# One shared set of 13 weight buffers with deeper splitting at the joints, and an in-place residual, in a two-block transformer kernel

## The chip, the cores and the metric

The kernel runs on one core of a Trainium2 chip. The metric is the device time of one execution in microseconds (us); the number given for a kernel is the median of several executions. The engines are named as in the profile: PE is TensorE (matrix multiplication), DVE is VectorE, ACT is ScalarE, POOL is GpSimd and SP is SyncE, whose queue issues the loads of the weights.

## The reference

256 tokens of width 1024 in float32 pass through two blocks. The joins between the stages are of two kinds: block 1 normalises after the sum (deep-norm, LayerNorm), block 2 normalises a branch with RMS, adds it, and normalises again ahead of the next branch.

```
block 1:  x = LN(alpha*x + retention(x));        x = LN(alpha*x + swiglu(x))
          x = LN(alpha*x + stick_breaking(x));   x = LN(alpha*x + moe_swiglu(x))   # 8 experts, top 2
block 2:  for l in 0, 1:
            x = x + RMS(hybrid_mixer_l(RMS(x)*mix_pre_g))*mix_post_g
            x = x + RMS(conv_ffn_l(RMS(x)*ffn_pre_g))*ffn_post_g
```

The time goes into the products with the weights: 519 MB of them, each used once.

## The kernel before

**Units.** Every weight matrix is cut into units of 1 MB (128 partitions x 2048 float32), numbered here U0 to U518 in the order of use: retention 0 to 31 (the last 8 are its output projection), ffn 32 to 64 (output projection from 54), stick-breaking attention 65 to 80, MoE 81 to 416, and then in block 2 hybrid mixer 0 (417 to 434), conv-ffn 0 (435 to 467, output projection from 457), hybrid mixer 1 (468 to 485) and conv-ffn 1 (486 to 518). To reach float32 accuracy a unit is used as two parts: SP loads the raw unit (`raw`, line 64), ACT copies it with rounding into `wh` (line 74), DVE subtracts to get the rest, `wl` (line 85), and PE forms three products, wh with xh, wl with xh, wh with xl, where xh and xl are the activation split in the same way (lines 191 and 192).

**The stream.** The class `Stream` keeps this going. Python code written in order decides which engine gets which instruction next; nothing is reordered later, and each engine, SP's queue among them, takes its instructions in that order. `get` hands PE the next split unit, `done` marks it as used, `advance` emits as many splits as allowed (at most `pairs` units split and not yet done) and as many loads as there are buffers. Raw units have 4 buffers of their own, split parts 8 (4 pairs; 3 pairs in the MoE, where further buffers are lent for raws).

**The joints.** `proj_out` (line 236) runs a stage's output projection, one unit after the other, with `advance` after each. Its last four units are the `tail` (line 248): all four for token half 0, then `joint.stats(0)`, then all four for token half 1, with `joint.trans(0)` ahead of the end, then `joint.stats(1)`. `stats(t)` adds and normalises the residual of a token half on DVE and ACT; `trans(t)` lets PE transpose it (line 1294), and ACT and DVE split it into xh and xl. `head` (line 269) then starts the next stage: four units for token half 0, with `trans(1)` ahead of the fourth, then the four for token half 1. So PE meets two places where it may have to wait: the head's first unit, which needs xh and xl of half 0, and `trans(1)`, which needs stats(1). In `tail` `advance` stands ahead of stats(0), after the units named in `joint.early`, and, where `joint.after` is set, behind stats(1).

The joint between retention and ffn is called ret to ffn, and so on: ffn to stick, stick to MoE, MoE to hyb0, hyb0 to conv-ffn0, conv-ffn0 to hyb1, hyb1 to conv-ffn1. The joints ret to ffn, ffn to stick, conv-ffn0 to hyb1 and the end come behind `proj_out`; the other stages call `tail` by themselves.

**The normalisations.** `LayerNorm.stats` (line 1317): z = alpha*x + acc and its statistics (lines 1326 and 1327), then per half of the columns z = (z - mean)*g and x = z*rs + b (1314, 1315), with rs from ACT's square root and DVE's reciprocal (317). `RmsNorm.stats` (line 1377): ACT squares acc (1384), then per column half z = acc*rs*g (1388) and x = z + x (1389); `pre` (1345) forms the next stage's input z. The residual x has two buffers that take turns.

Of the kernel before, what the change touches and what calls it, by code (L numbers as in the profile page):

```python
# [16 lines left out]
OP = mybir.AluOpType  # L17
# [15 lines left out]
class Stream:  # L33


    def __init__(self, nc, pool, pairs, raws, units):
        self.nc, self.pool, self.units = nc, pool, units
        self.pairs = self.room = pairs
        self.free = [(pool, "raw%d" % i, len(units)) for i in range(raws)]
        self.n_load = self.n_h = self.n_l = self.n_get = self.n_done = 0  # L40
        self.rt, self.ht = {}, {}

    def widen(self, slots):

        self.free = slots + self.free

    def slot(self):
        return next((s for s in self.free if self.n_load < s[2]), None)

    def raw(self, s):  # L50
        self.free.remove(s)
        if s[1] == "part":
            return s[0].tile([128, UNIT], F32, tag="part", name="raw", bufs=2 * self.room)
        return s[0].tile([128, UNIT], F32, tag=s[1], name="raw")

    def part(self, name):
        return self.pool.tile([128, UNIT], F32R, tag="part", name=name, bufs=2 * self.room)

    def load(self):
        s = self.slot()  # L60
        if s is None or self.n_load >= len(self.units):
            return False
        t = self.raw(s)
        self.nc.sync.dma_start(t, self.units[self.n_load])
        self.rt[self.n_load] = (t, s)
        self.n_load += 1
        return True

    def split_h(self):
# [3 lines left out]
        h = self.part("wh")  # L73
        self.nc.scalar.activation(h, self.rt[i][0], AF.Copy)  # L74
        self.ht[i] = h
        self.n_h += 1
        return True

    def split_l(self):
        i = self.n_l  # L80
        if i >= self.n_h:
            return False
        (r, s), h = self.rt.pop(i), self.ht[i]
        l = self.part("wl")
        self.nc.vector.tensor_tensor(l, r, h.bitcast(F32), op=OP.subtract)  # L85
        self.ht[i] = (h, l)
        self.free.append(s)
        self.n_l += 1
        self.load()
        return True  # L90

    def advance(self):
        while self.split_h():
            self.split_l()
        while self.split_l():
            pass
        while self.load():
            pass

    def get(self):  # L100
        i = self.n_get
# [5 lines left out]
        return self.ht.pop(i)  # L107

    def done(self):
        self.n_done += 1  # L110


# [10 lines left out]


class Net:
    PAIRS, RAWS = 4, 4

    def __init__(self, ctx, tc, a):
        self.ctx, self.tc, self.nc, self.a = ctx, tc, tc.nc, a

        def pool(name, bufs, **k):
            return ctx.enter_context(tc.tile_pool(name=name, bufs=bufs, **k))

        self.ring = pool("ring", 1)
        self.gl, self.xt, self.xT = pool("gl", 1), pool("xt", 1), pool("xT", 1)
        self.x_tag = 0
        self.sm = pool("sm", 2)
        self.ps = pool("ps", 1, space=PSUM)
        ctx.enter_context(tc.manual_schedule())

    def prepare(self, units):
        self.W = Stream(self.nc, self.ring, self.PAIRS, self.RAWS, units)

    def psA(self):
        return self.ps.tile([128, 2, 512], F32, tag="A", name="pa", bufs=2)
# [12 lines left out]
    def consts(self):  # L158
# [21 lines left out]
    def new_x(self):  # L180
        self.x_tag ^= 1
        self.x = self.xt.tile([128, 2, D], F32, tag="x%d" % self.x_tag, name="x")
        return self.x

    def new_xT(self):
        xh = self.xT.tile([128, KC, S], F32R, tag="xh", name="xh")
# [49 lines left out]
    def proj_out(self, yh, yl, n, joint):  # L236

        accs = [self.psA(), self.psA()]
        m = 4
        for u in range(n - m):  # L240
            w = self.W.get()
            for t in range(2):
                self.out_unit(accs[t], w, yh, yl, u, t, u == 0, False)
            self.W.done()
            self.W.advance()
        self.tail(accs, [(yh, yl, u) for u in range(n - m, n)], n == m, joint)

    def tail(self, accs, items, first, joint, hooks=()):
        m = len(items)
        ws = [self.W.get() for _ in range(m)]  # L250
        for i, (yh, yl, u) in enumerate(items):
            if i < len(hooks):
                hooks[i]()
            self.out_unit(accs[0], ws[i], yh, yl, u, 0, first and i == 0, i == m - 1)
        self.W.advance()
        joint.stats(0, accs[0])
        accs[1] = accs[1] or self.psA()
        for i, (yh, yl, u) in enumerate(items):
            self.out_unit(accs[1], ws[i], yh, yl, u, 1, first and i == 0, i == m - 1)
            self.W.done()  # L260
            if i == m - 2:
                joint.trans(0)
            if i in joint.early:
                self.W.advance()
        joint.stats(1, accs[1])
        if joint.after:
            self.W.advance()

    def head(self, joint, table, n=4):

        ws, ps = [], []
        for i in range(n):
            if i == n - 1:
                joint.trans(1)
                self.nc.scalar.preload_act_table_set(table + "_and_others")
            ws.append(self.get8())
            ps.append(self.psP([128, 2, 256]))
            self.tokB(ps[i], ws[i], 0)
        for i in range(n):
            self.tokB(ps[i], ws[i], 1)  # L280
            self.W.done()
            yield ps[i]
# [37 lines left out]
    def start(self):  # L320
        nc, a = self.nc, self.a
        self.xh, self.xl = self.new_xT()
        W = self.W
        sx, sw = W.free[:2]
        xr, t, h, l = W.raw(sx), W.raw(sw), W.part("wh"), W.part("wl")
# [9 lines left out]
        W.ht[0] = (h, l)  # L335
        W.free += [sx, sw]
        W.n_load = W.n_h = W.n_l = 1
        W.advance()
        nc.sync.dma_start(self.new_x(), a["x"])

    def rotary(self, ps, out, cos, sin, scale, pool):
        nc = self.nc
# [114 lines left out]
    def stick(self, joint0):  # L457
# [106 lines left out]
        between(6)  # L564
        parts(7)
        joint = LayerNorm(self, o, w, 2, "kT")
        joint.early = (0, 1, 2)
        joint.after = False

        def last():  # L570
            pv(6)
# [8 lines left out]
    def open_moe(self):  # L580

        W = self.W
        self.mp = p = self.span.enter_context(self.tc.tile_pool(name="m1", bufs=1))
        self.moe_i = i = W.n_get
        end = i + 6 * E * SL
        W.widen([(p, "yy", i + 44)] + [(p, "more%d" % j, end) for j in range(2)])
        while W.load():
            pass

    def moe(self, joint0):  # L590
        nc, tc, a, W = self.nc, self.tc, self.a, self.W
        with self.span:
            p, o = self.mp, self.shared
            end = self.moe_i + 6 * E * SL
            W.widen([(self.xt, "x%d" % (self.x_tag ^ 1), self.moe_i + 46)])
            W.load()
# [51 lines left out]
            W.widen([(self.ring, "part", end - 8)] * 2)  # L648
            while W.load():
                pass  # L650
            route(0)
            low_part(1, nc.vector)
            route(1)
# [193 lines left out]
            for st in [(e, s) for e in range(E) for s in range(SL)] + [None]:  # L847
# [19 lines left out]
                if prev is not None:  # L867
                    hh, hl = parts()
                    turn(prev[2], hh, hl)
                    if st is None:  # L870
                        joint = MoeNorm(self, o, p, 3, 0)
                        W.pairs = 4
                        W.advance()
                if st is not None and e in (1, 3, 5) and s > 4:
                    gather_step(e // 2 + 1, 2 * s - 10, True)
                if part is not None and s == 1:
                    if acc is None:
                        acc = self.new_x()
# [423 lines left out]
class LayerNorm(Joint):  # L1302
# [66 lines left out]
class RmsNorm(Joint, PreNorm):  # L1369
# [7 lines left out]
    def stats(self, t, acc):  # L1377
# [171 lines left out]
```

## Time and profile before

| what | value |
|---|---|
| median of 3 executions | 2299.37 us (2298.87 to 2300.28) |
| the profiled execution: time | 2301.24 us |
| its span in the profile | 2299.5 us |
| mean granted clock of TensorE | 0.986 of full speed |
| DMA: packets, bytes, mean rate | 80074, 562.07 MB, 244 GB/s |
| wl subtractions (DVE, line 85) | 518 |
| matrix instructions on PE | 13077 |

The span is the time from the first to the last instruction in the trace; the profiled execution's own time is 1.74 us longer and 1.87 us above the median. Rows of the trace give an instruction's start and its duration in us; in square brackets stands how long the engine was idle just before, and which instruction ended that. A mean granted clock of 1 would be 2.4 GHz all the time; where it falls, it falls to 1.2 GHz.

### The profile page before, as it was taken

The numbers are of one execution on the slowest core, as the hardware profiler recorded it, in microseconds if no ns is written. First come the engines' busy times: TensorE is split into PE (matmuls) and PEld (weight loads), VectorE is DVE, ScalarE is ACT, GpSimd is POOL, SyncE is SP. The second block draws the span as 40 slices with busy tenths as digits, with TensorE's granted clock in tenths as the row PEclk, the third lists the DMA queues.
The fourth block names the chain that finished last, engine by engine and source line by source line (L and its number), as shares of the span: only waits on it lengthen the run. The fifth ranks groups of instructions, "written<-read, shape, count | busy, mean of one in ns | idle before, by whom it ended". The sixth has DMA issues, their size and how long they took to land. (4 is left out here: it accounts for less than half of the span.)

```text
span 2299.5 us, 31879 instructions
## 1 busy us (share of the span) xinstructions
PE 2220.5 (97%) x13077; PEld 1929.2 (84%) x13077; DVE 1711.3 (74%) x1670; ACT 1373.2 (60%) x1376; POOL 88.1 (4%) x87
## 2 busy tenths in 40 slices
PE   8999999997999999999999999997999999999998
PEld 8998998886888888888887888886888998888996
DVE  6565554656889888888888888997876975776973
ACT  4343443474777777777776777774555654555652
POOL 4000000010000000000000000300000000000000
PEclk9999999998999999999999999998999999999999
DMA  8444555436989799989997999985334554433551
GB/s 317 147 165 165 184 195 189 151 115 256 366 333 340 284 388 352 357 312 383 351 361 284 354 370 363 356 328 179 129 125 151 203 185 163 149 129 129 212 193 65
DMA packets 80074, 562.07 MB, mean 244 GB/s; under 512 B 9072, under 2 KB 9136, under 8 KB 13488
## 3 DMA queue, kind: packets, MB, share of 16 engines
q1 hardware_dynamic: 76464, 547.39, 64.3%
q0 software_dynamic: 3456, 12.55, 1.6%
q8 instruction: 105, 1.72, 0.3%
q14 instruction: 49, 0.40, 0.1%
HBM read 558.86 MB, written 1.05 MB: 243 GB/s over the span
## 5 line engine op out<-in xcount | busy, mean ns | idle before, releaser
L85 DVE TENSOR_TENSOR wl<-raw,wh 128x2048 fp32r<-128x2048 f32 x518 | 1187.8, 2300 | 312.7 <-ACT wh L74 295.1
L74 ACT ACTIVATE wh<-raw 128x2048 fp32r<-128x2048 f32 x518 | 990.9, 1916 | 397.3 <-PE pp L744 198.5
L197 PE MATMUL pp<-xh,wh 128*128 128x256 f32 x1360 | 387.3, 285 | 7.8 <-ACT wh L191 7.8
L197 PE MATMUL pp<-xh,wl 128*128 128x256 f32 x1360 | 386.9, 285 | 1.2 <-DVE wl L85 1.1
L197 PE MATMUL pp<-xl,wh 128*128 128x256 f32 x1360 | 384.1, 282 | 0.0
L197 PEld LDWEIGHTS pp<-xh,wh 128*128 128x128 f32 x1360 | 257.8, 190 | 9.1 <-ACT wh L191 8.1
L197 PEld LDWEIGHTS pp<-xl,wh 128*128 128x128 f32 x1360 | 258.6, 190 | 0.2 <-issue 0.2
L197 PEld LDWEIGHTS pp<-xh,wl 128*128 128x128 f32 x1360 | 255.9, 188 | 2.4 <-DVE wl L85 1.4
L197 PE MATMUL pp<-wl,xh 128*128 128x256 f32 x720 | 207.0, 288 | 7.8 <-DVE wl L85 7.8
L197 PE MATMUL pp<-wh,xh 128*128 128x256 f32 x720 | 210.6, 292 | 3.4 <-DVE mix L1132 3.2
L197 PE MATMUL pp<-wh,xl 128*128 128x256 f32 x720 | 206.0, 286 | 0.0
L744 PE MATMUL pp<-wh,xgh 128*128 128x512 f32 x448 | 179.4, 400 | 3.7 <-DVEq L821 3.7
L744 PE MATMUL pp<-wh,xh 128*128 128x512 f32 x448 | 179.5, 401 | 0.0
L744 PE MATMUL pp<-wl,xh 128*128 128x512 f32 x448 | 178.0, 397 | 0.5 <-DVE wl L85 0.5
L744 PE MATMUL pp<-wl,xgh 128*128 128x512 f32 x448 | 176.6, 394 | 1.5 <-DVE wl L85 1.5
L744 PE MATMUL pp<-wh,xl 128*128 128x512 f32 x448 | 177.7, 397 | 0.0
L744 PE MATMUL pp<-wh,xgl 128*128 128x512 f32 x448 | 176.8, 395 | 0.0
L197 PEld LDWEIGHTS pp<-wl,xh 128*128 128x128 f32 x720 | 140.4, 195 | 9.8 <-DVE wl L85 8.8
L197 PEld LDWEIGHTS pp<-wh,xh 128*128 128x128 f32 x720 | 140.1, 195 | 5.8 <-issue 4.2
L754 PE MATMUL pa<-wh,hh 128*128 128x512 f32 x448 | 142.2, 399 | 0.7 <-ACT hh L191 0.7
L754 PE MATMUL pa<-wl,hh 128*128 128x512 f32 x448 | 141.4, 397 | 0.0
L754 PE MATMUL pa<-wh,hl 128*128 128x512 f32 x448 | 141.4, 397 | 0.0
(337 smaller groups left out, 3089.2 us busy)
## 6 DMA issues: line engine op xcount, KB each, us to landing
raw<-in_moe_w_in SPq DMA_DIRECT2D x224, 1024.0 KB, 6.8
raw<-in_moe_w_out SPq DMA_DIRECT2D x112, 1024.0 KB, 6.6
raw<-in_w_up SPq DMA_DIRECT2D x44, 1024.0 KB, 4.8
raw<-in_w_in SPq DMA_DIRECT2D x28, 1024.0 KB, 4.9
raw<-in_ret_w_in SPq DMA_DIRECT2D x23, 1024.0 KB, 5.2
raw<-in_ffn_w_in SPq DMA_DIRECT2D x22, 1024.0 KB, 4.9
raw<-in_w_down SPq DMA_DIRECT2D x22, 1024.0 KB, 4.8
raw<-in_ffn_w_out SPq DMA_DIRECT2D x11, 1024.0 KB, 4.8
```

What stands on the lines that cost most here:

```text
L74: self.nc.scalar.activation(h, self.rt[i][0], AF.Copy)
L85: self.nc.vector.tensor_tensor(l, r, h.bitcast(F32), op=OP.subtract)
L197: self.nc.tensor.matmul(out, lhsT=w, rhs=x, start=(i == 0), stop=(i == n - 1))
L744: nc.tensor.matmul(q, lhsT=x[:, k, :], rhs=ww[:, kk, :], start=(k == 0 and i == 0), stop=(k == KC - 1 and i == 2))
L754: nc.tensor.matmul(A[0][f], lhsT=x[:, k, :], rhs=ww[:, kk, half(f)], start=(s == 0 and k == 0 and i == 0), stop=(s == SL - 1 and k == 3 an ...
```

## The change

- The raws and the split parts take their buffers from one list of 13 equal ones; before there were 4 for raws and 8 for parts. A load is issued only if the buffers that are then left are enough for the splits that are still to come before it.
- In the plain stages up to 5 units may be split ahead (`PAIRS`), from the start of `proj_out` up to 6 (`JOINT_PAIRS`), and from the head's end of its first pass on 5 again; in the MoE 3 as before.
- `advance` stands after the tail's units 0, 1 and 2 at every joint; behind stats(1) only loads are issued.
- The residual is updated in its place. One buffer of x is given up; the MoE's sum has a buffer of its own instead.
- `LayerNorm.norm`: the reciprocal comes behind the first z. `RmsNorm.stats`: DVE multiplies acc by the weight g while ACT forms the squares, and one instruction per column half then does x = z*rs + x.

PE's instructions, their order, and the order of the loads stay as they are.

```diff
-        self.free = [(pool, "raw%d" % i, len(units)) for i in range(raws)]
+        self.free = [(pool, "b%d" % i, len(units)) for i in range(count)]
...
+    def take(self, i, name, dt=F32R):
+        s = next((s for s in self.free if i < s[2]), None)
+        assert s is not None
         self.free.remove(s)
+        return s[0].tile([128, UNIT], dt, tag=s[1], name=name), s
+
+    def spare(self, i):
+        return sum(i < s[2] for s in self.free)

     def load(self):
+        i = self.n_load
+        if i >= len(self.units):
             return False
+        parts = max(0, min(i - self.n_h + 1, self.pairs - (self.n_h - self.n_done)))
+        if self.spare(i) <= parts + (parts > 0):
+            return False
+        t = self.rt[i] = self.take(i, "raw", F32)
+        self.nc.sync.dma_start(t[0], self.units[i])
         self.n_load += 1
         return True
...
 class Net:
-    PAIRS, RAWS = 4, 4
+    PAIRS, JOINT_PAIRS, BUFS = 5, 6, 13
...
     def proj_out(self, yh, yl, n, joint):
         accs = [self.psA(), self.psA()]
+        self.W.pairs = self.JOINT_PAIRS
...
         joint.stats(1, accs[1])
-        if joint.after:
-            self.W.advance()
+        self.W.fill()
...
             self.tokB(ps[i], ws[i], 0)
+        self.W.pairs = self.PAIRS
...
 class Joint:
-    early = (0, 2)
-    after = True
+    early = (0, 1, 2)
...
-        self.xo = n.x
-        self.xn = n.new_x()
+        self.xo = self.xn = n.x
...
-        r = n.rstd(mv[:, 1:2], n.eps_ln, 1.0)
+        sd = n.small(1, "rs_sd")
+        nc.scalar.activation(sd, mv[:, 1:2], AF.Sqrt, bias=n.eps_ln)
+        r = n.small(1, "rs")
         for f in range(2):
             s = half(f)
             nc.vector.scalar_tensor_tensor(z[:, s], z[:, s], mv[:, 0:1], self.g[:, s], op0=OP.subtract, op1=OP.mult)
+            if f == 0:
+                nc.vector.reciprocal(r, sd)
             nc.vector.scalar_tensor_tensor(dst[:, s], z[:, s], r, self.b[:, s], op0=OP.mult, op1=OP.add)
...
-        nc.scalar.activation(z, acc, AF.Square, accum_out=ss)
+        nc.scalar.activation(junk, acc, AF.Square, accum_out=ss)
+        for f in range(2):
+            nc.vector.tensor_tensor(z[:, half(f)], acc[:, half(f)], self.g[:, half(f)], op=OP.mult)
         r = n.rstd(ss, n.eps_rms, 1.0 / D)
         for f in range(2):
             s = half(f)
-            nc.vector.scalar_tensor_tensor(z[:, s], acc[:, s], r, self.g[:, s], op0=OP.mult, op1=OP.mult)
-            nc.vector.tensor_tensor(self.xn[:, t, s], z[:, s], self.xo[:, t, s], op=OP.add)
+            nc.vector.scalar_tensor_tensor(self.xn[:, t, s], z[:, s], r, self.xo[:, t, s], op0=OP.mult, op1=OP.add)
```

**How the order of instructions moves.** Three places, all on DVE; a row is a line of the kernel, the operation, what it writes and reads, and how often it comes in succession. The lines of the change are some 3 to 8 higher (wl is line 85 before and 93 after, xl 192 and 196). First the joint ffn to stick on DVE, from the run of subtractions of the output projection to those behind stats(0); before:

```order
L85 TENSOR_TENSOR wl<-raw,wh 128x2048 x8
L1326 SCALAR_TENSOR_TENSOR z<-x,pa 128x512
L1327 BN_STATS st<-z 128x6
L1326 SCALAR_TENSOR_TENSOR z<-x,pa 128x512
L1327 BN_STATS st<-z 128x6
L1310 BN_AGGR mv<-st 128x2
L317 RECIPROCAL rs<-rs_sd 128x1
L1314 SCALAR_TENSOR_TENSOR z<-z,mv,gains 128x512
L1315 SCALAR_TENSOR_TENSOR x<-z,rs,gains 128x512
L1314 SCALAR_TENSOR_TENSOR z<-z,mv,gains 128x512
L1315 SCALAR_TENSOR_TENSOR x<-z,rs,gains 128x512
L85 TENSOR_TENSOR wl<-raw,wh 128x2048
```

The same place on DVE with the change:

```order
L93 TENSOR_TENSOR wl<-raw,wh 128x2048 x9
L1329 SCALAR_TENSOR_TENSOR z<-x,pa 128x512
L1330 BN_STATS st<-z 128x6
L1329 SCALAR_TENSOR_TENSOR z<-x,pa 128x512
L1330 BN_STATS st<-z 128x6
L1309 BN_AGGR mv<-st 128x2
L1315 SCALAR_TENSOR_TENSOR z<-z,mv,gains 128x512
L1317 RECIPROCAL rs<-rs_sd 128x1
L1318 SCALAR_TENSOR_TENSOR x<-z,rs,gains 128x512
L1315 SCALAR_TENSOR_TENSOR z<-z,mv,gains 128x512
L1318 SCALAR_TENSOR_TENSOR x<-z,rs,gains 128x512
L93 TENSOR_TENSOR wl<-raw,wh 128x2048 x2
```

The run ahead of stats(0) goes from U57 to U64 before and from U58 to U66 now, and two subtractions, U67 and U68, follow it where one stood; the reciprocal has moved behind the first z.

Second the head's side of the joint ret to ffn on DVE, from the end of stats(0) to the start of stats(1); before:

```order
L1315 SCALAR_TENSOR_TENSOR x<-z,rs,gains 128x512
L85 TENSOR_TENSOR wl<-raw,wh 128x2048
L192 TENSOR_TENSOR xl<-pp,xh 128x4x128 x2
L85 TENSOR_TENSOR wl<-raw,wh 128x2048 x2
L1326 SCALAR_TENSOR_TENSOR z<-x,pa 128x512
```

The same place on DVE with the change:

```order
L1318 SCALAR_TENSOR_TENSOR x<-z,rs,gains 128x512
L93 TENSOR_TENSOR wl<-raw,wh 128x2048 x2
L196 TENSOR_TENSOR xl<-pp,xh 128x4x128 x2
L93 TENSOR_TENSOR wl<-raw,wh 128x2048
L1329 SCALAR_TENSOR_TENSOR z<-x,pa 128x512
```

Ahead of xl, which the head's first unit needs, stand two subtractions (U34 and U35) where one stood (U32), and one (U36) stands ahead of stats(1) where U33 and U34 stood. Behind stats(1), where U35's subtraction stood ahead of the next xl, none is left. ACT's copies wh have moved in the same way.

Third the joint MoE to hyb0 on DVE, from the first subtraction behind stats(0) to the additions for token half 1 (x, or acc with the change, gathers the experts' sum); before:

```order
L85 TENSOR_TENSOR wl<-raw,wh 128x2048
L192 TENSOR_TENSOR xl<-pp,xh 128x4x128 x2
L85 TENSOR_TENSOR wl<-raw,wh 128x2048
L796 TENSOR_TENSOR x<-pp,x 128x512 x2
L1364 BN_STATS st<-x 128x6 x2
```

The same place on DVE with the change:

```order
L93 TENSOR_TENSOR wl<-raw,wh 128x2048
L196 TENSOR_TENSOR xl<-pp,xh 128x4x128 x2
L93 TENSOR_TENSOR wl<-raw,wh 128x2048 x3
L797 TENSOR_TENSOR acc<-pp,acc 128x512 x2
L1367 BN_STATS st<-acc 128x6 x2
```

Three subtractions stand ahead of the additions where one stood; the other two (the first splits of hyb0) have come from ahead of stats(0).

## Rows read from the trace of the kernel before

**Rows 1.** The page, part 1: busy time (us), share of the span, instructions.

```profile
PE 2220.5 (97%) x13077; PEld 1929.2 (84%) x13077; DVE 1711.3 (74%) x1670; ACT 1373.2 (60%) x1376; POOL 88.1 (4%) x87
```

**Rows 2.** Timeline of PE, output projection of ffn: start, duration, line, operation.

```profile
402.62 0.63 PE L233 MATMUL pa<-wl,yh 128*128 128x512 f32 x2
...
405.42 0.63 PE L233 MATMUL pa<-wl,yh 128*128 128x512 f32 x2
```

**Rows 3.** The page, part 5: count, then busy us, mean ns, idle before.

```profile
L85 DVE TENSOR_TENSOR wl<-raw,wh 128x2048 fp32r<-128x2048 f32 x518 | 1187.8, 2300 | 312.7 <-ACT wh L74 295.1
L74 ACT ACTIVATE wh<-raw 128x2048 fp32r<-128x2048 f32 x518 | 990.9, 1916 | 397.3 <-PE pp L744 198.5
```

**Rows 4.** Line 64, loads issued from 350 to 430 us, and timeline of SP.

```profile
DMA to landing us min/median/max: 4.7/4.8/5.6
...
362.75 0.33 SPq L64 DMA_DIRECT2D raw<-in_ffn_w_out  x1
```

**Rows 5.** Timeline of DVE, joint ffn to stick.

```profile
360.43 2.29 DVE L85 TENSOR_TENSOR wl<-raw,wh 128x2048 fp32r<-128x2048 f32 x1 [1.61 <-ACT wh L74]
...
403.75 0.69 DVE L1326 SCALAR_TENSOR_TENSOR z<-x,pa 128x512 f32<-128x512 f32 x1 [7.42 <-PE pa L233]
...
407.09 0.17 DVE L317 RECIPROCAL rs<-rs_sd 128x1 f32<-128x1 f32 x1 [0.36 <-ACT rs_sd L315]
...
410.08 2.28 DVE L85 TENSOR_TENSOR wl<-raw,wh 128x2048 fp32r<-128x2048 f32 x1
```

**Rows 6.** Timeline of ACT: first wh that a used unit releases in three output projections.

```profile
177.59 1.92 ACT L74 ACTIVATE wh<-raw 128x2048 fp32r<-128x2048 f32 x1 [1.29 <-PE pa L233]
...
358.49 1.92 ACT L74 ACTIVATE wh<-raw 128x2048 fp32r<-128x2048 f32 x1 [1.98 <-PE pa L233]
...
1885.62 1.92 ACT L74 ACTIVATE wh<-raw 128x2048 fp32r<-128x2048 f32 x1 [1.11 <-PE pa L233]
```

**Rows 7.** Timeline of PE, ffn to stick: head's first unit, U68.

```profile
415.65 0.28 PE L197 MATMUL pp<-wh,xh 128*128 128x256 f32 x1
...
428.56 0.58 PE L197 MATMUL pp<-wl,xh 128*128 128x256 f32 x1 [1.43 <-DVE wl L85]
```

**Rows 8.** Timeline of PE, ret to ffn: trans(0), head's first unit, U35.

```profile
214.26 1.04 PE L1294 MATMUL pp<-ident,x 128*128 128x128 f32 x8
...
217.95 0.28 PE L197 MATMUL pp<-wh,xh 128*128 128x256 f32 x1
...
230.87 0.58 PE L197 MATMUL pp<-wl,xh 128*128 128x256 f32 x1 [1.42 <-DVE wl L85]
```

**Rows 9.** Timeline of PE, conv-ffn0 to hyb1: head's first unit, U471.

```profile
1942.98 0.28 PE L197 MATMUL pp<-wh,xh 128*128 128x256 f32 x1
...
1955.85 0.39 PE L197 MATMUL pp<-wl,xh 128*128 128x256 f32 x1 [1.65 <-DVE wl L85]
```

**Rows 10.** Timelines of DVE and PE, MoE to hyb0: additions for half 1, trans(1).

```profile
1592.13 1.28 DVE L796 TENSOR_TENSOR x<-pp,x 128x512 f32<-128x512 f32 x2
...
1600.64 1.10 PE L1294 MATMUL pa<-ident,z 128*128 128x128 f32 x6 [2.60 <-DVE z L1345]
```

**Rows 11.** Timeline of PE, hyb0 to conv-ffn0: last matmul at pace, trans(1), U438.

```profile
1754.08 0.28 PE L197 MATMUL pp<-wh,xl 128*128 128x256 f32 x1
1755.41 1.38 PE L1294 MATMUL pa<-ident,z 128*128 128x128 f32 x8 [1.05 <-DVE z L1345]
1756.55 0.36 PE L197 MATMUL pp<-wh,xh 128*128 128x256 f32 x1
1758.55 0.39 PE L197 MATMUL pp<-wl,xh 128*128 128x256 f32 x1 [1.64 <-DVE wl L85]
```

**Rows 12.** Timeline of DVE at the end: the last addition of the residual.

```profile
2295.45 0.69 DVE L1389 TENSOR_TENSOR x<-z,x 128x512 f32<-128x512 f32 x1
```

**Rows 13.** Busy time by stretch: length, PE, PEld, DVE, ACT, POOL, PEclk, DMA share, GB/s.

```profile
214.00:240.00 26.00, 23.13 (x157) 21.81 (x156) 15.62 (x18) 9.85 (x10) 1.05 (x2) 0.87 0.54 203
...
420.00:440.00 20.00, 17.13 (x131) 16.49 (x130) 10.98 (x15) 8.38 (x9) 1.17 (x3) 0.91 0.43 159
```

More of the change, by code (lines that the diff above doesn't have):

```diff
@@ L33, with __init__, fill @@
 class Stream:
-    def __init__(self, nc, pool, pairs, raws, units):
-        self.nc, self.pool, self.units = nc, pool, units
-        self.pairs = self.room = pairs
-        self.free = [(pool, "raw%d" % i, len(units)) for i in range(raws)]
+    def __init__(self, nc, pool, pairs, count, units):
+        self.nc, self.units = nc, units
+        self.pairs = pairs
+        self.free = [(pool, "b%d" % i, len(units)) for i in range(count)]
         self.n_load = self.n_h = self.n_l = self.n_get = self.n_done = 0
-        self.rt, self.ht = {}, {}
+        self.rt, self.ht, self.held = {}, {}, {}
     def widen(self, slots):
         self.free = slots + self.free
-    def slot(self):
-        return next((s for s in self.free if self.n_load < s[2]), None)
-    def raw(self, s):
+    def take(self, i, name, dt=F32R):
+        s = next((s for s in self.free if i < s[2]), None)
+        assert s is not None
         self.free.remove(s)
[L52 to L57, printed above, removed]
+        return s[0].tile([128, UNIT], dt, tag=s[1], name=name), s
+    def spare(self, i):
+        return sum(i < s[2] for s in self.free)
     def load(self):
-        s = self.slot()
-        if s is None or self.n_load >= len(self.units):
-            return False
-        t = self.raw(s)
-        self.nc.sync.dma_start(t, self.units[self.n_load])
-        self.rt[self.n_load] = (t, s)
+        i = self.n_load
+        if i >= len(self.units):
+            return False
+        parts = max(0, min(i - self.n_h + 1, self.pairs - (self.n_h - self.n_done)))
[3 more added lines that the diff above has]
+        self.nc.sync.dma_start(t[0], self.units[i])
         self.n_load += 1
         return True
+    def fill(self):
+        while self.load():
+            pass
     def split_h(self):
@@ L72, in split_h @@
             return False
-        h = self.part("wh")
+        if self.spare(i) < 2:
+            return False
+        h, s = self.take(i, "wh")
         self.nc.scalar.activation(h, self.rt[i][0], AF.Copy)
-        self.ht[i] = h
+        self.ht[i], self.held[i] = h, [s]
         self.n_h += 1
@@ L82, in split_l @@
             return False
-        (r, s), h = self.rt.pop(i), self.ht[i]
-        l = self.part("wl")
+        l, s = self.take(i, "wl")
+        (r, raw), h = self.rt.pop(i), self.ht[i]
         self.nc.vector.tensor_tensor(l, r, h.bitcast(F32), op=OP.subtract)
         self.ht[i] = (h, l)
-        self.free.append(s)
+        self.held[i].append(s)
+        self.free.append(raw)
         self.n_l += 1
-        self.load()
         return True
     def advance(self):
-        while self.split_h():
+        n = self.n_load
+        while self.n_h < n and self.split_h():
             self.split_l()
@@ L96, in advance @@
             pass
-        while self.load():
-            pass
+        self.fill()
     def get(self):
@@ L109, in done @@
     def done(self):
+        self.free += self.held.pop(self.n_done)
         self.n_done += 1
@@ L135, in __init__ @@
         self.gl, self.xt, self.xT = pool("gl", 1), pool("xt", 1), pool("xT", 1)
-        self.x_tag = 0
         self.sm = pool("sm", 2)
@@ L141, in prepare @@
     def prepare(self, units):
-        self.W = Stream(self.nc, self.ring, self.PAIRS, self.RAWS, units)
+        self.W = Stream(self.nc, self.ring, self.PAIRS, self.BUFS, units)
     def psA(self):
@@ L178, in consts @@
         nc.vector.memset(self.eps_rms, RMS_EPS)
[L180 to L183, printed above, removed]
     def new_xT(self):
@@ L323, in start @@
         W = self.W
-        sx, sw = W.free[:2]
-        xr, t, h, l = W.raw(sx), W.raw(sw), W.part("wh"), W.part("wl")
+        (xr, sx), (t, sw) = W.take(0, "xr", F32), W.take(0, "raw", F32)
+        (h, sh), (l, sl) = W.take(0, "wh"), W.take(0, "wl")
         fh, fl = (x.rearrange("p k s -> p (k s)") for x in (self.xh, self.xl))
@@ L335, in start @@
         W.ht[0] = (h, l)
+        W.held[0] = [sh, sl]
         W.free += [sx, sw]
         W.n_load = W.n_h = W.n_l = 1
+        W.fill()
         W.advance()
-        nc.sync.dma_start(self.new_x(), a["x"])
+        self.x = self.xt.tile([128, 2, D], F32, name="x")
+        nc.sync.dma_start(self.x, a["x"])
     def rotary(self, ps, out, cos, sin, scale, pool):
@@ L566, in stick @@
         joint = LayerNorm(self, o, w, 2, "kT")
-        joint.early = (0, 1, 2)
-        joint.after = False
         def last():
@@ L585, in open_moe @@
         end = i + 6 * E * SL
-        W.widen([(p, "yy", i + 44)] + [(p, "more%d" % j, end) for j in range(2)])
-        while W.load():
-            pass
+        W.widen([(p, "yy", i + 44), (p, "acc", i + 46), (p, "more", end)])
+        W.fill()
     def moe(self, joint0):
@@ L594, in moe @@
             end = self.moe_i + 6 * E * SL
-            W.widen([(self.xt, "x%d" % (self.x_tag ^ 1), self.moe_i + 46)])
-            W.load()
             low, ones, slot = self.low[:, 0, :], self.low[:, 1, :], self.slot
@@ L647, in moe @@
             W.pairs = 3
-            W.widen([(self.ring, "part", end - 8)] * 2)
-            while W.load():
-                pass
+            W.fill()
             route(0)
@@ L871, in moe @@
                         joint = MoeNorm(self, o, p, 3, 0)
-                        W.pairs = 4
+                        W.pairs = self.PAIRS
                         W.advance()
@@ L877, in moe @@
                     if acc is None:
-                        acc = self.new_x()
+                        acc = p.tile([128, 2, D], F32, tag="acc", name="acc")
                     combine(*part, 0, True, e == 1)
@@ L1383, in stats @@
         ss = n.small(1, "ss")
-        nc.scalar.activation(z, acc, AF.Square, accum_out=ss)
+        junk = n.sm.tile([128, D], BF, tag="junk", name="junk", bufs=1)
+        nc.scalar.activation(junk, acc, AF.Square, accum_out=ss)
+        for f in range(2):
+            nc.vector.tensor_tensor(z[:, half(f)], acc[:, half(f)], self.g[:, half(f)], op=OP.mult)
         r = n.rstd(ss, n.eps_rms, 1.0 / D)
```

## The prediction

> **What bounds the kernel now.** The busy times come first: TensorE (PE) works for 2220.5 of the 2299.5 us, 97% [rows 1], so an edit pays only where PE stands still, and costs only where it makes PE stand still. Next the pace: in a projection PE takes two matmuls of 512 columns every 0.47 us. From 402.62 to 405.42 are 12 of them, half a unit in 2.80 us, so a unit takes 5.6 us [rows 2]. Then the weight stream: a unit costs ScalarE (ACT) 1.92 us (wh) and VectorE (DVE) 2.30 us (wl) [rows 3], and its load takes 4.7 to 5.6 us, 4.8 as a rule, from issue to landing; a load goes out 0.03 us after the subtraction that frees its buffer (the one at 360.43 ends at 362.72, the load starts at 362.75) [rows 4, 5]. Last I read PE's waits at the joints, where the normalisation between two stages sits.
>
> **The buffers.** Before, four raws and four pairs are apart: up to four loads run ahead. After, 13 buffers serve all. In the plain stages five pairs leave three for raws: three units of 5.6 us cover a load with its copy and subtraction, 9.1 us, so I cost them at nothing; without the cover a unit would cost up to 3.5 more. From proj_out on six pairs are allowed and take 12; one buffer is left. A raw then waits until the subtraction of the unit before it has read that same buffer, and load, copy and subtraction of successive units run one after another: 0.03 + 4.85 + 1.92 + 2.30 = **9.1 us a unit** [rows 3, 4], against PE's 5.6. This holds for raws U32 to U36 and beyond, U62 to U69, U465 to U472. And the orders of ACT and DVE put two splits ahead of stats(0), two ahead of the head's xh/xl, one ahead of stats(1); ACT and DVE take work in order, so a split that waits for its load holds up the joint behind it.
>
> The Trainium skill, "Trainium Kernel Development and Optimization", section Best Practices, asks for double buffering so that loads overlap with compute; one buffer for raws is against it. By that rule, with a second raw in flight, the period would fall to what ACT and DVE need, under 5.6 us, and the three joints below would cost nothing.
>
> **ffn to stick, worked out.** U54 is used up when ACT starts wh at 358.49 [rows 6]. Then U59: wh to 360.4, wl to 362.7; U60's wh to 364.6, wl to 367.0; U61's wl to 369.3. U62 is the first in the single buffer: wl at 378.4, then 387.5, 396.6 (U64, which PE needs about 4 us later: no stall), 405.7, and U66 at 414.8. Only then may stats(0) start, which began at 403.75. It took 6.3 us to the next subtraction [rows 5] and saves about 0.35 by the reciprocal that now stands behind the first z (it waited 0.36 for ACT): x is ready at 420.8. U67 is split at 423.9, U68 at 433.0, xl's first half is there at 433.7. PE starts the head at about 433.5 instead of 415.65 [rows 7]. U69's wl ends at 442.1, stats(1) at 448.1, the transposes of trans(1) 0.6 later: U68 begins at 448.7 instead of 428.56 [rows 7]. **+20.2**.
>
> **ret to ffn.** From U24's release at 177.59 [rows 6] the same steps give wl of U31 at 188.3, U32 197.4, U33 206.5: half a microsecond late for stats(0), which PE does not feel, for it reaches trans(0) at 214.26 [rows 8]. U34 goes to 215.6, U35 to 224.5, xl's first half to 225.2; the head starts at 225 instead of 217.95 [rows 8]. U36 is ready at 233.5, stats(1) at 239.5, PE at 240.1 instead of 230.87 [rows 8]. **+9.2**.
>
> **conv-ffn0 to hyb1.** U457's release at 1885.62 [rows 6] gives U464 at 1896.4, U469 at 1941.9, stats(0) to 1947.8 (with the multiplication by the weight beside the squares), U470 1951.0, U471 1960.1, head 1960.6 instead of 1942.98 [rows 9]; U472 1969.2, stats(1) 1975.1, PE 1975.7 instead of about 1955.7 [rows 9]. **+20.0**.
>
> The Trainium skill, "DMA: Bandwidth & Descriptors", section Anatomy of one DMA, fits a transfer as 2.0 us plus its bytes at 436 GB/s. For 1 MB that is an estimated 4.4 us, 0.4 less than the row; over the 21 periods in the three joints the sum would be about 8 us lower. The row decides.
>
> **MoE to hyb0.** Two splits that stood before stats(0) now follow it: three instead of one between xl and the additions for token half 1. They start two subtractions later than at 1592.13 (+4.5), less 0.35 for the reciprocal; PE reaches trans(1) that much later than 1600.64, where it already waits 2.60 for z [rows 10]. **+4.0**; from below 0, if ACT and DVE find time earlier, from above 4.6.
>
> **hyb0's first features.** Two splits stand ahead of the second rotation's ro; one subtraction more, 2.3 [rows 3]. It shows in no wait of before: 0 to 2.3, I take **+2.3** since PE waits for ro right there.
>
> **What is gained.** hyb0 to conv-ffn0 has five pairs, its splits are done before stats(1): the idle times of 1.05 before trans(1) and 1.64 before the next wl, with the slow first matmuls around them, go: 1754.20 (end of the pace) to 1755.41 is 1.2, 1756.55 to 1758.55 less one matmul 1.9, and 0.3 at the transposes [rows 11]. **−3.4**. hyb1 to conv-ffn1 shows the same pattern: **−3.4**. stick to MoE has two hidden reciprocals, **−0.4**. At the end the weight is multiplied before rs is there, and of z, x, z, x two steps are left behind it; the two additions of 0.69 go [rows 12]: **−1.4**. DVE's lost z-x steps at other RMS joints lie inside the waits above. The in-place residual I cost at nothing: each half is read by z on the same engine before it is written, and PE's transposes of it come later; if one had to wait, it would be for one half, 0.8.
>
> **Clock.** Around the two early joints the granted clock is 0.87 over 26 us and 0.91 over 20 us [rows 13], that is 3.4 and 1.7 us lost (half speed, the lower level of 1.2 GHz, for 6.8 and 3.4 us). The new stops should again be followed by such stretches, partly inside the next wait: I take **−1.7** in all, from −7 to +12.
>
> **Sum.** 9.2 + 20.2 + 20.0 + 4.0 + 2.3 − 3.4 − 3.4 − 0.4 − 1.4 − 1.7 = +45.4. The profiled execution took 2301.24 us (span 2299.5), 1.9 above the median of 2299.37; on the median this is **2345 us**. No change means within 0.2% (4.6 us), about what a measurement of this kernel can tell.
>
> **Rivals.**
> *Faster* (7 in 100). The loads aren't tied to one buffer, because a free one turns up that I count as taken, or the splits come early enough. It decides when a unit's period is 5.6 us or less, so with a load of 1.3 us in one buffer, or with two raws. Then the two early joints also lose their last waits (1.42 before U35's wl, 1.43 before U68's [rows 7, 8], 3.4 each with trans(1)'s), conv-ffn0 to hyb1 as much, and half the clock's loss goes: −10.2 − 8.6 (the gains above) − 2 + 6.3 = −14.5, **2285**. Against it: 4.7 us is the shortest load in the rows [rows 4]. The second raw is what the Trainium skill, "Trainium Kernel Development and Optimization", section Best Practices, would have; this order has none there.
> *It doesn't bite* (4 in 100). The chain runs, but with so short a lead that the joints end where they ended, and gains and MoE joint cancel: **2299**. That needs both: an early start of splits and a queue that lets the joint by. The order has them in one queue.
> *One unit less* (9 in 100). One more raw was loaded before the reserve closed to a single buffer, so that each of the long chains has a period less: −9.1 at two joints, **2327**. For it: three raws are held when proj_out starts. Against: the counts of buffers give U32, U62 and U465 as the first.
> *Clock* (14 in 100). Each of the six new stops (7 to 18 us long) is followed by a stretch at half speed that no wait hides; at 1.7 to 3.4 us each that is 10 to 20, less 5 that stood already: **2355**. For it: [rows 13], where stops of only 3.4 us did it.
> The forecast itself has 66 in 100.
>
> **Range.** Forecast, the shorter chain and most of the clock case, with the bounds of loads (21 periods by 0.2 either way, 4 us) and of the MoE joint: 2326 to 2358. Slower 66 + 14 + 9 = 89 in 100, same 4, faster 7.
>
> **What would show it.** On DVE at ffn to stick, subtractions 9.1 us apart from about 369 to 415, each behind a wh that waits for a DMA; loads of SP that wait for wl and land 4.8 later; stats(0) 11 us late; PE idle for about 7, 10 and 6 us there, and almost as long at conv-ffn0 to hyb1; at hyb0 to conv-ffn0 no wait for wl. I am wrong if subtractions come at PE's pace of 5.6 us through the joints, or if PE starts the stick head at about 416.

## The result and the profile after

The changed kernel takes **2371.01 us** (median of 4 executions, 2368.18 to 2373.47) against 2299.82 for the kernel before beside it: a ratio of 1.0308 with a 95% interval of 1.029 to 1.0326. The forecast was 2345, with a range up to 2358: the direction was right, the size was not. It lost 71 us where 45 were forecast.

PE issues the same 13077 matrix instructions in the same order in both kernels, so each one has a delay: its start after, less its start before. The growth of that delay over a stage is what the stage lost. This table is worked out that way from the traces; the forecast's term stands beside it, and two experiments (e3 and e8) to which the text comes below. A row reaches to the start of the next one. The forecast's −1.4 at the end and −1.7 for the clock stand in no row.

| stage (from, us before) | forecast | change | e3 | e8 |
|---|---|---|---|---|
| start (6) and retention (60) | 0 | +1.6 | +0.3 | −0.2 |
| ret to ffn (205) | +9.2 | +9.3 | −6.2 | −6.2 |
| ffn (245) | 0 | 0.0 | +1.4 | 0.0 |
| ffn to stick (402) | +20.2 | +22.3 | −4.9 | −4.9 |
| stick (445) | 0 | 0.0 | +0.1 | +0.4 |
| stick to MoE (545) | −0.4 | −0.6 | −0.6 | −0.6 |
| MoE (566) | 0 | **+15.6** | +1.4 | +2.5 |
| MoE to hyb0 (1560) | +4.0 | +3.4 | +3.7 | +1.3 |
| hyb0 (1606) | +2.3 | +0.6 | −2.1 | +0.7 |
| hyb0 to conv-ffn0 (1735) | −3.4 | −4.8 | −4.8 | −4.8 |
| conv-ffn0 (1766) | 0 | **+3.3** | +3.3 | 0.0 |
| conv-ffn0 to hyb1 (1925) | +20.0 | +20.5 | −0.8 | −0.8 |
| hyb1 (1970) | 0 | +1.0 | −0.4 | −0.4 |
| hyb1 to conv-ffn1 (2085) | −3.4 | −3.2 | −3.2 | −3.2 |
| conv-ffn1 (2115) | 0 | **+1.8** | +3.3 | 0.0 |

The joints came out within about 2 us. Between them, where the forecast had nothing, 22 us were lost.

The busy times of the changed kernel, from the part of the page that answers to [rows 1]:

```profile
PE 2232.5 (94%) x13077; PEld 1939.9 (82%) x13077; DVE 1710.2 (72%) x1670; ACT 1373.6 (58%) x1376; POOL 89.9 (4%) x87
```

The span is 70.1 us longer (2369.6), yet DVE and ACT have as much work as before. PE is busy 12.0 us longer with the same instructions, at a lower granted clock (mean 0.974 against 0.986); the rest is waiting.

The timeline of DVE at the joint ffn to stick in the changed kernel, which answers to [rows 5]:

```profile
387.79 2.29 DVE L93 TENSOR_TENSOR wl<-raw,wh 128x2048 fp32r<-128x2048 f32 x1 [6.94 <-ACT wh L82]
396.92 2.29 DVE L93 TENSOR_TENSOR wl<-raw,wh 128x2048 fp32r<-128x2048 f32 x1 [6.83 <-ACT wh L82]
406.22 2.29 DVE L93 TENSOR_TENSOR wl<-raw,wh 128x2048 fp32r<-128x2048 f32 x1 [7.01 <-ACT wh L82]
415.41 2.29 DVE L93 TENSOR_TENSOR wl<-raw,wh 128x2048 fp32r<-128x2048 f32 x1 [6.90 <-ACT wh L82]
426.86 2.29 DVE L93 TENSOR_TENSOR wl<-raw,wh 128x2048 fp32r<-128x2048 f32 x1 [9.16 <-ACT wh L82]
429.07 0.68 DVE L1329 SCALAR_TENSOR_TENSOR z<-x,pa 128x512 f32<-128x512 f32 x1
...
436.01 2.29 DVE L93 TENSOR_TENSOR wl<-raw,wh 128x2048 fp32r<-128x2048 f32 x1 [0.88 <-ACT wh L82]
445.23 2.29 DVE L93 TENSOR_TENSOR wl<-raw,wh 128x2048 fp32r<-128x2048 f32 x1 [6.92 <-ACT wh L82]
...
454.37 2.29 DVE L93 TENSOR_TENSOR wl<-raw,wh 128x2048 fp32r<-128x2048 f32 x1 [5.65 <-ACT wh L82]
```

U62 to U69 come 9.1 to 9.3 us apart, the forecast 9.1. Only between U65 and U66 are there 11.45: the load of U66 was issued at 417.7 and took 7.1 us to land instead of 4.85. These 2.2 us are as much as the 2.1 by which the joint lost more than forecast.

The timeline of ACT there shows what the copies wait for, and the timeline of PE what that costs (PE's first two rows are the halves of trans(0), the third is the head's first unit, the fourth is trans(1)):

```profile
385.84 1.92 ACT L82 ACTIVATE wh<-raw 128x2048 fp32r<-128x2048 f32 x1 [7.90 <-DMA raw<-in_ffn_w_out]
394.97 1.92 ACT L82 ACTIVATE wh<-raw 128x2048 fp32r<-128x2048 f32 x1 [7.21 <-DMA raw<-in_ffn_w_out]
```

```profile
433.74 1.11 PE L1293 MATMUL pp<-ident,x 128*128 128x128 f32 x4 [10.62 <-DVE x L1318]
435.19 1.12 PE L1293 MATMUL pp<-ident,x 128*128 128x128 f32 x4 [0.34 <-DVE x L1318]
445.74 0.58 PE L201 MATMUL pp<-wh,xh 128*128 128x256 f32 x1 [4.71 <-ACT xh L195]
...
461.25 0.66 PE L1293 MATMUL pa<-ident,x 128*128 128x128 f32 x4 [1.93 <-DVE x L1318]
```

The head starts at 445.74 where it started at 415.65 [rows 7], 30.1 later, of which 11.0 had been lost before the joint.

In the MoE PE waits at four places, near 790 to 815, 1059 to 1071, 1261 to 1274 and 1583. Its delay grows there by 6.5, 5.6, 4.0 and 2.6 us; between them some 3 come back. Here are the timelines of ACT and of DVE at the first, and the waits of ACT over the whole MoE (us in total, times, longest):

```profile
787.77 1.92 ACT L82 ACTIVATE wh<-raw 128x2048 fp32r<-128x2048 f32 x1 [1.88 <-DVE wl L93]
792.05 5.52 ACT L82 ACTIVATE wh<-raw 128x2048 fp32r<-128x2048 f32 x3 [2.36 <-DVE wl L93]
```

```profile
785.45 2.29 DVE L93 TENSOR_TENSOR wl<-raw,wh 128x2048 fp32r<-128x2048 f32 x1 [0.48 <-ACT wh L82]
...
789.72 2.29 DVE L93 TENSOR_TENSOR wl<-raw,wh 128x2048 fp32r<-128x2048 f32 x1 [1.39 <-ACT wh L82]
...
793.99 6.70 DVE L93 TENSOR_TENSOR wl<-raw,wh 128x2048 fp32r<-128x2048 f32 x3 [1.98 <-ACT wh L82]
```

```profile
ACT wh L82 <- PE pp L745: 194.0, 196, 8.4
...
ACT wh L82 <- DVE wl L93: 21.9, 9, 3.3
```

The copy at 787.77 starts when the subtraction of the unit before it ends (785.45 + 2.29 = 787.74); that unit's own subtraction waits for the copy; the next copy at 792.05 waits for that. ACT and DVE take turns, 4.28 us a unit. Nine copies wait so, and PE pays (timeline of PE, at the first place):

```profile
796.34 0.50 PE L745 MATMUL pp<-wl,xgh 128*128 128x512 f32 x1 [0.78 <-DVE wl L93]
...
809.49 0.50 PE L745 MATMUL pp<-wl,xgh 128*128 128x512 f32 x1 [1.75 <-DVE wl L93]
...
814.76 0.50 PE L745 MATMUL pp<-wl,xgh 128*128 128x512 f32 x1 [2.21 <-DVE wl L93]
```

The addresses that the two programs give their buffers say why. As a rule a part of the MoE lies where a part of three units before lay, which PE has done with. At the four places this is broken in two ways. At U146, U147, U152, U154, U234, U300 and U405 `wh` is laid into the buffer of the raw unit just before, which that unit's subtraction gives back; these are the turns above. (It is so at U114 and U119 too, where PE lost nothing.) And at U233, U299 and U404 `wh` is laid into that of the `wh` two units before, which PE still reads; at U151 and U153 it is a `wl` two units before. The timeline of ACT at the second place has both, U232 to U235:

```profile
1048.59 1.92 ACT L82 ACTIVATE wh<-raw 128x2048 fp32r<-128x2048 f32 x1 [0.89 <-PE pp L745]
...
1054.59 1.92 ACT L82 ACTIVATE wh<-raw 128x2048 fp32r<-128x2048 f32 x1 [2.20 <-PE pp L745]
1058.87 3.71 ACT L82 ACTIVATE wh<-raw 128x2048 fp32r<-128x2048 f32 x2 [2.36 <-DVE wl L93]
```

The copy of U233 starts 6.0 us after the one before it, that of U234 another 4.28 later, where 2.8 is the pace: the wait for PE is the larger part here. What breaks the rotation is that the MoE lends buffers for a time. In the program of the change parts lie in them too. The loan of `xh` and `xl` ends with U150, those of `oh` and `ol` with U148, U232, U298 and U402; at each of the four places the two that come free may not be used any more, the loads hold the rest, and the next split goes out a unit later. Why it breaks at U146 and U147 already stays open. In the kernel before, which keeps raws and parts apart but for two buffers of parts that the MoE lends to raws, U156 is the only unit of the MoE whose `wh` lies in the buffer of the raw just before, and one copy waits so (waits of ACT over the MoE, before):

```profile
ACT wh L74 <- DVE wl L85: 1.4, 1, 1.4
```

In conv-ffn0 PE waits 2.2 us behind the head. The timelines of PE and of ACT there, of the change:

```profile
1824.90 0.66 PE L302 MATMUL pp<-ident,fl 128*128 128x128 f32 x4 [2.19 <-ACT fl L295]
```

```profile
1820.67 3.69 ACT L82 ACTIVATE wh<-raw 128x2048 fp32r<-128x2048 f32 x2
1824.28 0.58 ACT L295 ACTIVATE fl<-pp 128x512 f32<-128x512 f32 x1
```

Two copies go out in one `advance`, since five pairs let them; the small copy `fl`, on which PE waits, stands behind both.

### The profile page after: what moved, and what is told of

It is laid out like the page before. It is cut to its first block, busy times and chain, and to the rows that moved or that the text cites. A ratio compares the mean times of both kernels' runs of the same rounds, so it can differ in the third digit from the quotient of the medians.

```text
span 2369.6 us, 31845 instructions
## 1 busy us (share of the span) xinstructions
PE 2232.5 (94%) x13077; PEld 1939.9 (82%) x13077; DVE 1710.2 (72%) x1670; ACT 1373.6 (58%) x1376; POOL 89.9 (4%) x87
## 5 line engine op out<-in xcount | busy, mean ns | idle before, releaser
L201 PEld LDWEIGHTS pp<-wh,xl 128*128 128x128 f32 x720 | 141.8, 197 | 6.2 <-DVE xl L196 6.2
```

Of the source, the lines that this page charges most:

```text
L201: self.nc.tensor.matmul(out, lhsT=w, rhs=x, start=(i == 0), stop=(i == n - 1))
```

## The experiments

In the order of the runs. e2, e3 and e5 to e8 hold one more edit, which is called *kinds apart* below: the 13 buffers stay in one list, but a part takes first a buffer that `done` gave back, a raw one that a subtraction gave back.

**e1, five pairs at the joints**

```diff
-    PAIRS, JOINT_PAIRS, BUFS = 5, 6, 13
+    PAIRS, JOINT_PAIRS, BUFS = 5, 5, 13
```

> The change with JOINT_PAIRS 5 instead of 6, all else as changed: three buffers stay for raws at the joints. Theory A (at the joints the raws share one buffer, 9.1 us a unit): the losses at ret to ffn, ffn to stick and conv-ffn0 to hyb1 (together 9.3 + 22.3 + 20.5 = 52 us between the two traces) go, and these joints even gain the last wait that they had before, some 3 each: 2371 - 52 - 9 = about 2310. Rival B (the splits that stand ahead of the joint's work in ACT's and DVE's queues cost it, whatever the buffers): the three joints keep half or more of their loss, 2340 or above. In both the MoE's 15.5 us of loss and those of the conv-ffn stages stay.

Measured: 2307.56 us, ratio to before 1.0018 (1.0005 to 1.0031). The three joints went from +9.3, +22.3 and +20.5 to −6.2, −4.9 and −0.8, as theory A has it. The MoE kept 15.8, conv-ffn 0 and 1 lost 3.3 each. The start, whose instructions are the same in both, lost nothing here: its 1.6 in the profiled execution of the change is not the change's. Five pairs also move splits in the queues, so e1 alone does not separate A from B; e5 to e7 do.

**e2, kinds apart, with six pairs at the joints**

```diff
     def done(self):
-        self.free += self.held.pop(self.n_done)
+        self.free += self.held[self.n_done]
+        self.used += self.held.pop(self.n_done)
...
-        s = next((s for s in self.free if i < s[2]), None)
+        ok = [s for s in self.free if i < s[2]]
+        s = next((s for s in ok if (s in self.used) == (name != "raw")), ok[0])
+        if s in self.used:
+            self.used.remove(s)
```

> The change with JOINT_PAIRS 6, but a split part takes first a buffer that a used unit (PE) gave back, and a raw first one that a subtraction (DVE) gave back; the 13 buffers stay shared. Theory C (in the MoE some wh land in the buffer that the subtraction of the unit just before gives back, so ACT's copy and DVE's subtraction take turns, 4.3 us a unit against PE's 2.8): the stalls of the MoE go, 13 to 16 us less than the change, 2355 to 2358. Rival D (the MoE waits for its weights: fewer loads ahead after the late joints): the MoE keeps its loss, 2368 or above. The three joints keep theirs in both.

Measured: 2372.04 us, ratio to before 1.03 (1.0278 to 1.0321): as slow as the change, and by its total a miss. By stages it is not what D says: the MoE's loss fell from 15.6 to 2.7. What was won there was lost elsewhere: 1.7 in the retention (unexplained), 4.7 in ffn, 5.3 in stick, 2.4 more in hyb1. In ffn the timeline of DVE shows it:

```profile
257.00 2.29 DVE L95 TENSOR_TENSOR wl<-raw,wh 128x2048 fp32r<-128x2048 f32 x1 [1.38 <-ACT wh L84]
...
266.13 2.29 DVE L95 TENSOR_TENSOR wl<-raw,wh 128x2048 fp32r<-128x2048 f32 x1 [5.60 <-ACT wh L84]
```

9.13 us once more: the single buffer for raws lasts a unit longer behind the joint, where the change has a subtraction at 261.74.

**e3, kinds apart, and five pairs at the joints**

> Both edits of the two runs before at once. If theories A and C are right, they add up: 2371 - 61 - 15 = about 2295, that is a little faster than before, with what is left of the cost in MoE to hyb0, hyb0's features and the conv-ffn stages (together some 10 us) against the gains of the joints. If B and D are right, 2335 or above.

Measured: 2291.54 us, ratio 0.9954 (0.9938 to 0.9971): faster than before, and 16 less than e1. The edit from e1 to e3 touches only the choice of buffers; the MoE's loss fell from 15.8 to 1.4, at the four places from 6.5, 5.6, 4.0 and 2.5 to 0.2, 0.2, 0.0 and 0.0. In e3's program each `wh` from U90 on to the MoE's end lies where that of three units before lay, and as no buffer is missing, some splits (U128, U154, U236, U302 among them) go out a place earlier than in e1. The timeline of ACT at the first of the four places, and the waits of ACT in the MoE, in which DVE is no longer named:

```profile
741.20 1.92 ACT L84 ACTIVATE wh<-raw 128x2048 fp32r<-128x2048 f32 x1 [0.86 <-DMA raw<-in_moe_w_in]
...
744.01 1.92 ACT L84 ACTIVATE wh<-raw 128x2048 fp32r<-128x2048 f32 x1 [0.42 <-PE pa L758]
746.83 1.92 ACT L84 ACTIVATE wh<-raw 128x2048 fp32r<-128x2048 f32 x1 [0.90 <-PE pa L758]
749.61 1.92 ACT L84 ACTIVATE wh<-raw 128x2048 fp32r<-128x2048 f32 x1 [0.86 <-PE pp L748]
```

```profile
ACT wh L84 <- PE pp L748: 193.9, 209, 3.1
ACT wh L84 <- PE pa L758: 76.5, 99, 1.6
```

A copy comes every 2.8 us. Theory C holds in that the choice of buffers costs the MoE its 14 us; but the turns of ACT and DVE, which it names, are only one of the two ways, and no run parts them.

**e4, the arithmetic of the joints alone**, on the kernel before: the diff's lines in `LayerNorm.norm` and `RmsNorm.stats`, nothing else.

> The kernel before with the new arithmetic of the joints alone: the reciprocal behind the first z in LayerNorm; in RmsNorm the product with the weight beside the squares and one step per half for x. Buffers, pairs and places of the splits as before. By the prediction's terms: 1.4 at the end, 0.4 to 0.5 at stick to MoE, 0.35 twice at MoE to hyb0, some tenths at each joint whose stats(1) PE waits for: 3 to 5 us faster than before, 2295 to 2297. If nothing of the normalisation is on the path but the end: 2298.

Measured: 2298.17 us, ratio 0.9984 (0.9971 to 0.9996). By stages, at the joints: −1.4, −1.6, −0.5 (stick to MoE), −2.2 (MoE to hyb0), −0.6, +1.2 and +1.0 (the two late RMS joints, unexplained), +0.5 in the MoE and +0.4 in hyb0, and +0.75 at the start, whose code is unchanged; in all −2.3 until PE's last matmul and −0.6 behind it. These 3 us are the low end of the 3 to 5 expected, with 0.6 at the end instead of 1.4. The new arithmetic is a small gain.

**e5, e6, e7: one, two or three raws at a joint, with the splits in the same places.** Kinds apart, and

```diff
-    PAIRS, JOINT_PAIRS, BUFS = 5, 6, 13
+    PAIRS, JOINT_PAIRS, BUFS = 4, 5, 13
```

in e5, with 12 in place of 13 in e6, and 11 in e7.

> As e3 (parts and raws keep to the buffers of their kind), with 4 pairs in the plain stages and 5 at the joints behind proj_out, 13 buffers: three for raws at those joints, five elsewhere. By theory E (in the conv-ffn heads and the MoE's end the fifth pair puts two splits in one go ahead of small ACT and DVE work) the conv-ffn stages and hyb0's features cost nothing and MoE to hyb0 half of its 3.5; the joints ret to ffn, ffn to stick and conv-ffn0 to hyb1 gain as in e3 (6.2, 4.9, 0.8); hyb0 to conv-ffn0 and hyb1 to conv-ffn1 lose their gain of 3 to 5 each, since the pairs are 4 there. About 10 to 12 us faster than before.

> e5 with 12 buffers: two for raws at the joints behind proj_out, and the same places of the splits there. Theory A: two raws in turn give a unit every 9.1/2 = 4.6 us, under PE's 5.6, so these joints stay within 2 us of e5. In the MoE one buffer less is lent to loads: 0 to 5 us slower.

> e5 with 11 buffers: one for raws at the joints behind proj_out, and again the same places of the splits. Theory A: a unit every 9.1 us, so ret to ffn, ffn to stick and conv-ffn0 to hyb1 are worse than e5 by about 15, 27 and 21 us, that is back at the losses of the change (+9, +22, +20 against before). Rival B (the places of the splits decide, not the number of raws): as e5 within 3 us. The MoE may lose some us by two buffers less in either case.

Measured: e5 2300.17 us (ratio 0.9995, 0.9986 to 1.0004), e6 2312.6, e7 2387.73 (one execution each). By its total e5 is a miss: no faster than before, where 10 to 12 us were expected. By stages, before as zero:

| stage | e5, 3 raws | e6, 2 raws | e7, 1 raw |
|---|---|---|---|
| ret to ffn, and ffn behind it | −6.2, 0.0 | −1.9, +0.7 | +9.2, +12.8 |
| ffn to stick, and stick | −4.9, 0.0 | −2.2, 0.0 | +13.5, +4.4 |
| conv-ffn0 to hyb1, and hyb1 | −3.2, 0.0 | +1.2, +1.5 | +22.0, +4.0 |
| conv-ffn 0 and 1 | 0.0, 0.0 | 0.0, 0.0 | 0.0, +9.1 |
| hyb0 to conv-ffn0, hyb1 to conv-ffn1 | +4.4, +5.8 | +3.9, +5.9 | +4.3, +4.8 |

The timelines of DVE in the output projection of ffn, of e6 and then of e7:

```profile
382.48 2.29 DVE L95 TENSOR_TENSOR wl<-raw,wh 128x2048 fp32r<-128x2048 f32 x1 [2.79 <-ACT wh L84]
388.08 2.29 DVE L95 TENSOR_TENSOR wl<-raw,wh 128x2048 fp32r<-128x2048 f32 x1 [3.31 <-ACT wh L84]
393.68 2.29 DVE L95 TENSOR_TENSOR wl<-raw,wh 128x2048 fp32r<-128x2048 f32 x1 [3.31 <-ACT wh L84]
```

```profile
401.37 2.29 DVE L95 TENSOR_TENSOR wl<-raw,wh 128x2048 fp32r<-128x2048 f32 x1 [7.01 <-ACT wh L84]
410.50 2.29 DVE L95 TENSOR_TENSOR wl<-raw,wh 128x2048 fp32r<-128x2048 f32 x1 [6.84 <-ACT wh L84]
419.62 2.29 DVE L95 TENSOR_TENSOR wl<-raw,wh 128x2048 fp32r<-128x2048 f32 x1 [6.83 <-ACT wh L84]
```

With two raws 5.60 us a unit, PE's own pace; with one 9.13. The places of the splits are the same in all three, but for a few instructions at ffn's head in e7 (255 to 264 us), so rival B falls. The single buffer is what costs; the order in the queues turns that into a wait of the joint. e6 lost 4.4 at most at a joint against e5, not the 2 expected. The table shows two things more. In e7 parts of the loss lie in the stage behind the joint: of the 12.8 in ffn, 4.9 arose at its head and 7.9 in its output projection, where PE waits 4.2 us for a copy `wh`, for with one pair less than in the change PE ran out of split units before the tail's end. The 9.1 of conv-ffn1 lie in its output projection too. And four pairs cost nothing in conv-ffn0 with three raws (e7, plain stages) as with five (e5), so the 3.3 of the change came from the fifth pair and not from fewer raws. The last row is where e5 missed: with four pairs these two joints do not fall back to before, they lose 4 to 6 against it; why stays open.

**e8, four pairs where two splits in one go hurt**, on e3:

```diff
-        self.W.pairs = self.PAIRS
+        self.W.pairs = 4 if table in ("gelu_apprx_tanh", "silu") else self.PAIRS
...
-                        W.pairs = self.PAIRS
+                        W.pairs = 4
```

> e3 with 4 pairs after the heads of ffn and conv-ffn and at the MoE's end, and 5 elsewhere and from proj_out on, 13 buffers. Theory E: of e3's terms +1.4 (ffn), +3.3 and +3.3 (conv-ffn 0 and 1) go and MoE to hyb0 falls from +3.7 to about +1.5, all gains of the joints stay: 10 us less than e3, about 2281, 0.8% faster than before. Rival: if those costs come from the five pairs' fewer raws and not from two splits in one go, the conv-ffn stages keep them and it ends at 2288 or above.

Measured: **2285.45 us**, ratio 0.9933 (0.9919 to 0.9946), the fastest of all. conv-ffn 0 and 1 and ffn lost nothing any more, MoE to hyb0 1.3 instead of 3.7; hyb0 lost 2.9 and the MoE 1.1 against e3, unexplained, which keeps it from 2281. The timeline of ACT in conv-ffn0:

```profile
1761.44 1.90 ACT L84 ACTIVATE wh<-raw 128x2048 fp32r<-128x2048 f32 x1
1763.24 0.57 ACT L298 ACTIVATE fl<-pp 128x512 f32<-128x512 f32 x1
1763.72 1.01 ACT L1252 ACTIVATE u<-pp,cw 128x256 f32<-128x256 f32 x2
```

One copy, then `fl`: theory E holds, and its rival, the fewer raws, fell with e7. Around the two early joints the granted clock no longer falls, as in e1 and e3 already (busy time by stretch, columns as in [rows 13]):

```profile
214.00:240.00 26.00, 26.00 (x211) 25.36 (x210) 14.31 (x20) 9.69 (x13) 1.05 (x2) 1.00 0.51 163
410.00:440.00 30.00, 29.29 (x248) 29.05 (x247) 17.71 (x18) 14.13 (x14) 1.17 (x3) 1.00 0.54 184
```

## Why the prediction was wrong in size

**Right: the single buffer at the joints.** The period of 9.1 us, the units it holds for, the joints ret to ffn (+9.2 forecast, +9.3 measured), ffn to stick (+20.2, +22.3, the difference about one slow load) and conv-ffn0 to hyb1 (+20.0, +20.5). e7 against e5 and e6 shows that it is the number of raws. PE's waits at ffn to stick are 11.0 us ahead of trans(0), 6.3 at the head and 2.7 ahead of trans(1), where about 7, 10 and 6 were named: the sum is near, the split is not.

**Near in size: the smaller joints.** MoE to hyb0 +4.0 (its own terms give 4.15) against +3.4; hyb0 to conv-ffn0 −3.4 against −4.8; hyb1 to conv-ffn1 −3.4 against −3.2; stick to MoE −0.4 against −0.6. hyb0's features lost less than the +2.3 taken: +0.6 over the stage, with other shifts in it. At the end −0.6 (span against PE's last matmul) for the −1.4 forecast. MoE to hyb0 came near partly by luck: e4 gives −2.2 there for the arithmetic alone, where the forecast counted 0.35, so if the two add up, the splits cost about 5.6 and not 4.5.

**Wrong: what lies between the joints was put at nothing.** Of the plain stages the forecast said: "five pairs leave three for raws: three units of 5.6 us cover a load with its copy and subtraction, 9.1 us, so I cost them at nothing". That step asked only whether a load comes in time. For the MoE, 994 us long, the sum has no term and the text no reason. Missed were a way in which the common list acts and one in which the fifth pair acts:

- In the MoE parts now take lent buffers, and where a loan ends `wh` lands in a buffer that PE still reads, or in the one that the subtraction just before gives back. The copy then comes 6.0 us after the last one (U233), or ACT and DVE take turns, 4.28 us, against 2.8, and PE lost **15.6**. e1 against e3 shows it as the choice of the buffers; what each of the two ways costs is not shown apart.
- In the conv-ffn heads the fifth pair puts two copies in one go ahead of a small copy that PE needs: **+3.3 and +1.8** in the change, 3.3 twice in e1 and e3, nothing in e8. The forecast had counted splits ahead of small work at the joints and at hyb0, but not there.

15.6 + 5.1 are 20.7 of the 25 us that were missing between the spans (70.1 for 45.4); the slow load is about 2.1, and the start 1.6, which is not the change's.

**The rivals and the range.** None of the rivals was this. The forecast of a clock term of −1.7 cannot be seen apart: the granted clock was lower around the late joints of the change (0.78 from 420 to 475 us), yet these joints lost what the chain alone predicts, so most of it probably lay inside waits; no run sets the clock's share apart. The range to 2358 was built from rivals and bounds that all sat at the joints; for the MoE's thousand microseconds it had none. The in-place residual, put at nothing, was not tried alone.

**The rule on double buffering** (the Trainium skill, "Trainium Kernel Development and Optimization", Best Practices). The trace of e6 agrees: a second raw in flight brings the unit back to PE's pace, 5.60 us.

**The time of a load.** The fit in the Trainium skill, "DMA: Bandwidth & Descriptors", Anatomy of one DMA, is given there for DMAs that GpSimd issues, and these loads are issued by SP. Its estimated 4.4 us for 1 MB would have made the chain 8.7. The trace has 4.8 and 9.13 to 9.30, and the measurement decides.

## What to carry to other kernels

When buffers are pooled, trace for every stage which instruction frees the buffer that the next one takes: a pool can make one engine wait for another that it ran beside, without a single instruction more. Buffers that join the pool for a time call for this most, at the end of their loan. A deeper reserve of split units is taken from the loads' buffers: at three joints 6 pairs and 1 raw cost 52 us, 5 pairs with 2 raws gained 3 (e6), and 5 pairs with 3 raws gained 12 (e3). A stage costed at nothing needs a bound too, the wider the longer the stage.

## What was not expected of the hardware

One load of 1 MB out of the eight at ffn to stick took 7.1 us from issue to landing with nothing else of the weights under way, where the median there was 4.8; in this chain of single loads it shifted what stood behind it by nearly its whole excess. The DMA queues in its time (417.7 to 425) show one thing more than those of its neighbours:

```profile
q8 instruction: 1, 0.02, 1.1%
```

A packet of 16 KB on the queue for instructions starts 0.1 us after the load was issued, and no other single load at the three joints has such a packet in its first 4 us. Of this load, six packets of 8 KB still follow one another from 422.6 to 424.5, when all others had ended by 422.1. That this packet delayed them is likely but not shown; no run kept the two apart.
